# Strassen partial results accumulated in PSUM banks, mixer weights of layer 0 split ahead in gate and up, sums of squares on GpSimd: a two-layer hybrid decoder trunk

## The chip, the cores and the metric

One core of one Trainium2 chip. The metric is device time of one execution in microseconds (us), the median over several runs; lower is better. Float32 inputs and outputs.

## The reference

```python
for l in range(DEPTH):                      # DEPTH = 2, x is 512 tokens x 1024
    x = x + 0.5 * swiglu(rmsnorm(x, ffn1_norm[l]), ffn1_w_gate[l], ffn1_w_up[l], ffn1_w_down[l])
    proj = rmsnorm(x, mix_norm[l]) @ w_in[l]
    # four token mixers on column groups of proj: GLA, RG-LRU, RWKV-7, Mamba-2
    x = x + concatenate([y_gla, y_lru, y_rw, y_ssd]) @ w_out[l]
    x = x + 0.5 * swiglu(rmsnorm(x, ffn2_norm[l]), ffn2_w_gate[l], ffn2_w_up[l], ffn2_w_down[l])
return rmsnorm(x, final_norm)
# swiglu(x, g, u, d) = (silu(x @ g) * (x @ u)) @ d, 1024 -> 2816 -> 1024
```

## The kernel before, in words

The activations stay transposed: features on the 128 partitions, the 512 tokens along the free axis. The program is a straight line of FFN (0,0), mixers 0, FFN (0,1), FFN (1,0), mixers 1, FFN (1,1). Every large product is made of two 16-bit parts of each float32 operand, a rounded f16 part and a bf16 residue, in three matmuls (hi·hi, hi·lo, lo·hi). Splitting a weight tile takes an ACT cast (L245, f16) and a DVE subtraction (L214, bf16 residue).

**Gate and up** (`ffn`, L606). The 2816 hidden columns are cut in `NP` = 11 pairs of 128-column blocks. A pair `n`, for gate and up at once, is a 2x2 Strassen-Winograd product: seven half-size products of 24 matmuls of 128x256 (`product`, L564) in place of eight. Their operands are the weight blocks and sums of them: a11, a12, a22, s1, s2, s3, s4. The sums s1 and s3 come out of an accumulating DMA that GpSimd issues (`load_sums`, L532, tile `rb`); s2 and s4 are DVE additions in place in `ra`; `form` (L547) splits each into a tile `q`, of which there are `NQ` = 5. The activation operands `xf` are made once (`prep_forms`, L437).

Results lie in PSUM banks: `A` (a11, then a12 added by TensorE), `D` (a22), `B` (s2), `C` (s3), `E` (s1, then s4 added by TensorE). DVE forms the rest: `u2` = B − M1 (L722, M1 being an ACT copy of A after a11, L690), `u3` = u2 + C (L737), and the quarters of the tile `S`: u3 + D (L738), u3 + E (L679) and −E − u2 (`finish12`, L645). Then the row scale R, SiLU on ACT, the product and the split of `h`.

R comes from the sum of squares of x: eight ACT squares and seven DVE additions `acc<-acc,sq` (`prep_sum`, L460), a matmul with ones (`ns`), a power on GpSimd (`rtm`, L254), four transposes (`nb`) and an ACT copy to `R`. It runs beside the first products of an FFN.

**Down**: 16 half products of 33 matmuls of 128x512. Their weights `w` are loaded by SP, split into `ws` and used one tile later (`w_next`, L405). In its loop a generator `side` is advanced (L782): `pieces(l)` (L411) loads 512 columns of a mixer weight tile (`pw`), splits them (`ps`) and stores both parts to DRAM (`w_scr`), four pieces for each tile named in `AHEAD[l]`, the first two steps being loads alone. Such a tile is later loaded ready for use; the others are split in the mixers (`w_split`, L377) with two 128x1024 casts and subtractions.

**Mixers** (`mixers`, L1610): 17 weight tiles (`small`, `w1` to `w12` of the input projection, `w13` to `w16` of the output projection). Six generators and a `tail` of projections are interleaved at build time by a modelled `Clock` (L97) and the table `PACE`; a list scheduler then fixes each engine's order. `pre_ffn` (L575) loads and splits the first blocks of the next FFN. All engines run their own queue in order.

Of the kernel before, what the change touches and what calls it, by code (L numbers as in the profile page):

```python
# [35 lines left out]
AHEAD = (range(8, 15), range(3, 15))  # L36
# [130 lines left out]
def kernel(ctx: ExitStack, tc: tile.TileContext, xT, wffn, wmain, wdown, wsmall, pv_d, pr_d, sm_d, cn_d, outT):  # L167
# [292 lines left out]
    def prep_sum(k):  # L460
        if k == ORDER[0]:
            acc["t"] = slot("acc")
            ACT(acc["t"], x[k], AF.Square)
        else:
            s = slot("sq")
            ACT(s, x[k], AF.Square)
            TT(acc["t"], acc["t"], s, ADD)
# [138 lines left out]
    def ffn(l, ph, what, mid=None, keep=False, side=None, ahead=0):  # L606
# [5 lines left out]
        A, B, C, D, E, M1, U2, U3, S = {}, {}, {}, {}, {}, {}, {}, {}, {}  # L612
# [31 lines left out]
        def finish12(n):  # L644
            STT(quarter(n, 0, 1), gu(E.pop(n)), -1.0, gu(U2.pop(n)), MUL, SUB)  # L645
            scale_gate(n, 0)

        def sums(ks):
            for k in ks:
                prep_sum(k)  # L650

        for n in range(NP):
# [21 lines left out]
            if n == 1 and s == 0:  # L674
                R = norm_spread(r)
            A[n] = fbank("A")
            product(A[n], n, "a11", 0)
            if n - 1 in E:
                TT(quarter(n - 1, 1, 1), gu(U3.pop(n - 1)), gu(E[n - 1]), ADD)  # L679
                form(n - 1, "s4")  # L680
            if n == 0:
                load_sums(s, 1)
# [4 lines left out]
            D[n] = fbank("D")  # L687
            product(D[n], n, "a22", 3)
            M1[n] = slot("m1")
            acopy(out=M1[n], in_=A[n])  # L690
            if n > 0:
                scale_gate(n - 1, 1)
                activate(n - 1, 1, False)
            form(n, "a12")
            if n - 1 in E:
                product(E[n - 1], n - 1, "s4", 2, start=False)
            form(n, "s2")
            product(A[n], n, "a12", 1, start=False)
# [5 lines left out]
            if n == 0:  # L704
                sums(ORDER[0:4])
            B[n] = bank("B")
            product(B[n], n, "s2", 5)
            S[n] = wp.tile([128, 2048], F32, tag="w", name="S")
            acopy(out=quarter(n, 0, 0), in_=gu(A.pop(n)))
# [4 lines left out]
            if n == 0:  # L714
                sums(ORDER[4:8])
                r = norm_sum(1.0 / SX)
            if n == 2 and mid is not None:
                mid()
            C[n] = bank("C")
            product(C[n], n, "s3", 6)  # L720
            U2[n] = slot("u2")
            TT(U2[n], B.pop(n), M1.pop(n), SUB)  # L722
            if n + 2 < NP:
                load_sums(s, n + 2)
            elif not last:
                st["stage"] = s
                w_fill(stops[s] - 1, stops[s])
            if not last:
                form(n + 1, "a11")
            else:  # L730
                w_fill(stops[s], stops[s] + 1)
            E[n] = bank("E")
            product(E[n], n, "s1", 4)
            if n == 0:
# [1128 lines left out]
```

## Time and profile before

| | us |
|---|---|
| three runs | 1895.6, 1888.79, 1894.05 |
| median | 1894.05 |
| profiled execution | 1888.55 |
| its span, first to last instruction | 1886.8 |

| stage, us from the span's start | length | TensorE busy | VectorE busy |
|---|---|---|---|
| FFN (0,0), pairs 1 to 10: 49.81 to 226.10 | 176.29 | 176.29 | 163.73 |
| FFN (0,0), down: 230.59 to 344.18 | 113.59 | 112.67 | 65.46 |
| mixers of layer 0: 344.18 to 630.46 | 286.28 | 266.30 | 209.38 |
| mixers of layer 1: 1283.46 to 1546.88 | 263.42 | 260.73 | 195.78 |

The span is what the instructions of the profile cover; the execution's own time is 1.75 us more. Busy times are sums over instructions, and neighbours of a pipelined engine overlap a little, so an engine's instructions can start closer together than they last. In a row of the trace, the bracket at the end is the idle time ahead of it on its engine and what ended it. PE is TensorE, DVE VectorE, ACT ScalarE, POOL GpSimd, SP SyncE.

### The profile page before, as it was taken

The numbers are of one execution on the slowest core, as the hardware profiler recorded it, in microseconds if no ns is written. First come the engines' busy times: TensorE is split into PE (matmuls) and PEld (weight loads), VectorE is DVE, ScalarE is ACT, GpSimd is POOL, SyncE is SP. The second block draws the span as 40 slices with busy tenths as digits, with TensorE's granted clock in tenths as the row PEclk, the third lists the DMA queues.
The fourth block names the chain that finished last, engine by engine and source line by source line (L and its number), as shares of the span: only waits on it lengthen the run. The fifth ranks groups of instructions, "written<-read, shape, count | busy, mean of one in ns | idle before, by whom it ended". The sixth has DMA issues, their size and how long they took to land.

```text
span 1886.8 us, 33473 instructions
## 1 busy us (share of the span) xinstructions
PE 1811.9 (96%) x13758; PEld 1263.4 (67%) x13846; DVE 1463.4 (78%) x2389; ACT 901.3 (48%) x1404; POOL 77.2 (4%) x77
## 2 busy tenths in 40 slices
PE   6999999899998899999999999999999999999997
PEld 3888844346855588884468887444577558888544
DVE  8999964577877899996679998554777789999733
ACT  7555543443243655555455555444223456555520
POOL 0000000000000000000000000000000000000000
PEclk9999999899999999999999999999999999999999
DMA  8777367522142667736867672773212256774331
GB/s 299 207 207 211 90 216 259 195 90 78 31 138 63 196 181 211 199 111 223 269 214 217 192 207 92 223 261 136 89 37 68 101 145 192 212 203 131 108 108 45
DMA packets 113386, 304.43 MB, mean 161 GB/s; under 512 B 34512, under 2 KB 56016, under 8 KB 98128
## 3 DMA queue, kind: packets, MB, share of 16 engines
q1 hardware_dynamic: 107040, 257.19, 40.7%
q0 software_dynamic: 6192, 45.09, 12.4%
q8 instruction: 108, 1.77, 0.4%
q14 instruction: 46, 0.38, 0.1%
HBM read 272.87 MB, written 29.38 MB: 160 GB/s over the span
## 4 chain that ended last, share of the span: by engine, by line
PE 77%; DVE 9%; DMA 4%; issue 4%; ACT 4%; POOL 1%; SPq 1%; POOLq 0%; DVEq 0%; ACTq 0%
PE d L192 18%; PE A L192 11%; PE E L192 11%; PE pj L192 10%; PE C L192 5%; PE D L192 5%; PE B L192 5%; PE pt L192 3%; DMA w<-in_wdown_dram 2%; DVE ws L214 1%; DVE q L214 1%; PE wo L192 1%; DMA pw<-in_wmain_dram 1%; PE z L192 1%; PE go L192 1%
## 5 line engine op out<-in xcount | busy, mean ns | idle before, releaser
L192 PEld LDWEIGHTS <-q 128*128 128x128 f16 (+1 forms) x7320 | 717.0, 98 | 140.9 <-ACT q L245 24.5
L192 PEld LDWEIGHTS <-ws 128*128 128x128 f16 (+1 forms) x2802 | 274.5, 98 | 329.7 <-issue 23.1
L192 PE MATMUL d<-h,ws 128*128 128x512 f16 (+3 forms) x2135 | 456.6, 372 | 3.8 <-ACT h L245 1.6
L245 ACT CAST q<-ra 128x1024 f16<-128x1024 f32 (+1 forms) x177 | 181.6, 1030 | 209.2 <-PE E L192 110.8
L192 PE MATMUL A<-xf,q 128*128 128x256 f16 (+1 forms) x2064 | 244.8, 274 | 15.6 <-ACT q L245 10.6
L192 PE MATMUL E<-xf,q 128*128 128x256 f16 x2064 | 239.4, 273 | 3.3 <-DVE S L214 3.3
L214 DVE TENSOR_TENSOR ws<-w,ws 128x640 bf16<-128x640 f32 (+3 forms) x222 | 148.9, 710 | 92.6 <-ACT ws L245 91.6
L245 ACT CAST ws<-w 128x640 f16<-128x640 f32 (+3 forms) x222 | 127.6, 633 | 190.8 <-DMA w<-in_wdown_dram 69.3
L214 DVE TENSOR_TENSOR q<-ra,q 128x1024 bf16<-128x1024 f32 (+1 forms) x177 | 211.8, 1199 | 4.7 <-ACT q L245 4.6
L214 DVE TENSOR_TENSOR q<-rb,q 128x1024 bf16<-128x1024 f32 x88 | 107.5, 1223 | 31.1 <-ACT q L245 31.1
L192 PE MATMUL D<-xf,q 128*128 128x256 f16 (+1 forms) x1032 | 122.6, 273 | 2.5 <-ACT q L245 2.1
L192 PE MATMUL B<-xf,q 128*128 128x256 f16 (+1 forms) x1032 | 121.8, 274 | 1.1 <-ACT q L245 1.1
L192 PE MATMUL C<-xf,q 128*128 128x256 f16 (+1 forms) x1032 | 119.7, 273 | 0.0
L192 PEld LDWEIGHTS <-w 128*128 128x128 f16 (+1 forms) x672 | 64.3, 99 | 80.7 <-issue 14.1
L245 ACT CAST q<-rb 128x1024 f16<-128x1024 f32 x88 | 91.8, 1047 | 24.0 <-PE D L192 19.3
L192 PE MATMUL pj<-xh,w 128*128 128x512 f16 x320 | 102.0, 380 | 1.2
L192 PE MATMUL pj<-xh,ws 128*128 128x512 f16 x288 | 92.9, 393 | 5.6 <-ACT xh L241 4.9
L218 DVE SCALAR_TENSOR_TENSOR dx<-d,R 128x512 f32<-128x512 f32 (+1 forms) x33 | 22.2, 673 | 78.2 <-PE d L192 78.2
L241 ACT ACTIVATE th<-S 128x512 f32<-128x512 f32 x88 | 55.5, 631 | 47.4 <-DVE S L214 47.3
L536 POOL DMA_DIRECT2D rb<-in_wffn_dram x43 | 37.8, 880 | 806.1 <-DVE h L214 324.9
L214 DVE TENSOR_TENSOR ps<-pw,ps 128x512 bf16<-128x512 f32 x76 | 50.0, 687 | 26.4 <-ACT ps L245 24.7
L214 DVE TENSOR_TENSOR h<-hf,h 128x512 bf16<-128x512 f32 x88 | 57.9, 684 | 8.2 <-ACT h L245 8.2
(343 smaller groups left out, 2280.1 us busy)
## 6 DMA issues: line engine op xcount, KB each, us to landing
w<-in_wdown_dram SPq DMA_DIRECT2D x64, 704.0 KB, 4.2
ra<-in_wffn_dram SPq DMA_DIRECT2D x87, 512.0 KB, 4.8
rb<-in_wffn_dram SPq DMA_DIRECT2D x43, 1024.0 KB, 5.0
rb<-in_wffn_dram POOLq DMA_DIRECT2D x43, 1024.0 KB, 9.9
rc<-in_wffn_dram SPq DMA_DIRECT2D x43, 512.0 KB, 8.7
pw<-in_wmain_dram SPq DMA_DIRECT2D x76, 256.0 KB, 5.1
w_scr<-ps SPq DMA_DIRECT2D x76, 256.0 KB, 4.1
w<-w_scr SPq DMA_DIRECT2D x19, 1024.0 KB, 4.8
```

The lines of the kernel that those rows point to most:

```text
L192: PE.matmul(out, lhsT, rhs, start=start, stop=stop, skip_group_check=free)
L214: V.tensor_tensor(out=out, in0=in0, in1=in1, op=op)
L218: V.scalar_tensor_tensor(out=out, in0=in0, scalar=scalar, in1=in1, op0=op0, op1=op1)
L241: A.activation(out=out, in_=in_, func=func, scale=scale, bias=bias)
L245: A.copy(out=out, in_=in_)
L536: nc.gpsimd.dma_start(out=t, in_=wffn[s, n, :, 3072:5120], accum_op=ADD)
```

## The change

**Sums in banks.** Four banks are kept for a whole FFN: two for B (by n mod 2), one each for C and D. Four matmuls of 128x512 open them once per FFN. Then ACT copies −A (after a11) into B, on which TensorE adds s2; ACT copies B into C, on which s3 is added; C into D, on which a22 is added; and s4 is added on B, in the next pair. s1 goes into a bank of its own, which ACT copies to SBUF (`m5`). D is copied by ACT into its quarter of S. DVE keeps two of its five sums a pair, C + m5 and −B − m5. Counted from both programs for 43 pairs: 129 DVE additions of 128x512 fewer; 43 more each of the ACT copies C<-B, D<-C, S<-D, m<-E, while B<-A takes the place of m<-A. The order of the products changes, and a22 of a pair is formed inside its pair; since `pre_ffn` and the start of FFN (0,0) form it as well, it is formed twice in four places.

**Splits ahead.** `AHEAD[0]` grows by the tiles 3 to 7: 20 more pieces (load, ACT cast, DVE residue, store), 10 fewer casts and 10 fewer residues of 128x1024 in the mixers of layer 0, and five loads out of `w_scr`. In gate and up of FFN (0,0) `side` is advanced twice a pair, in those of FFN (1,0) once; 31 steps are left for the down of (0,0) (30 before), 12 for that of (1,0) (22 before).

**Sums of squares.** The seven additions at each FFN's start go from DVE to GpSimd; the 20 others stay.

Besides, small loads and derived constants move to other pairs, and `pre_ffn` runs earlier in the mixers.

```diff
-AHEAD = (range(8, 15), range(3, 15))
+AHEAD = (range(3, 15), range(3, 15))
...
-    def prep_sum(k):
+    def prep_sum(k, pool=False):
         if k == ORDER[0]:
             acc["t"] = slot("acc")
             ACT(acc["t"], x[k], AF.Square)
         else:
             s = slot("sq")
             ACT(s, x[k], AF.Square)
-            TT(acc["t"], acc["t"], s, ADD)
+            if pool:
+                GP.tensor_tensor(out=acc["t"], in0=acc["t"], in1=s, op=ADD)
+            else:
+                TT(acc["t"], acc["t"], s, ADD)
...
 
         def finish12(n):
-            STT(quarter(n, 0, 1), gu(E.pop(n)), -1.0, gu(U2.pop(n)), MUL, SUB)
+            STT(quarter(n, 0, 1), gu(B[n % 2]), -1.0, gu(E.pop(n)), MUL, SUB)
...
         def sums(ks):
             for k in ks:
-                prep_sum(k)
+                prep_sum(k, pool=True)
...
+            if n == 0:
+                load_sums(s, 1)
             A[n] = fbank("A")
+            if B is None:
+
+                B, C, D = [bank("B"), bank("B")], bank("C"), bank("D")
+                h, X = qs[n, "a11"][0], xf[0][0]
+                for t in (*B, C, D):
+                    mm(t, h[:, 0, 0:128], X[:, 0:2].rearrange("p n t -> p (n t)"))
             product(A[n], n, "a11", 0)
             if n - 1 in E:
-                TT(quarter(n - 1, 1, 1), gu(U3.pop(n - 1)), gu(E[n - 1]), ADD)
-                form(n - 1, "s4")
-            if n == 0:
-                load_sums(s, 1)
+                acopy(out=quarter(n - 1, 1, 0), in_=gu(D))
+                TT(quarter(n - 1, 1, 1), gu(C), gu(E[n - 1]), ADD)
+            form(n, "s2")
             if not last:
                 load_blocks(s, n + 1)
             else:
                 w_fill(stops[s] - 1, stops[s] + 1)
-            D[n] = fbank("D")
-            product(D[n], n, "a22", 3)
-            M1[n] = slot("m1")
-            acopy(out=M1[n], in_=A[n])
+            if n - 1 in E:
+                product(B[(n - 1) % 2], n - 1, "s4", 2, start=False)
+            ACT(B[n % 2], A[n], AF.Copy, scale=-1.0)
             if n > 0:
                 scale_gate(n - 1, 1)
-                activate(n - 1, 1, False)
             form(n, "a12")
-            if n - 1 in E:
-                product(E[n - 1], n - 1, "s4", 2, start=False)
-            form(n, "s2")
-            product(A[n], n, "a12", 1, start=False)
+            product(B[n % 2], n, "s2", 5, start=False)
             form(n, "s3")
             if n - 1 in E:
                 finish12(n - 1)
             elif n > 0:
                 scale_gate(n - 1, 0)
-            if n == 0:
+            if n > 0:
+                activate(n - 1, 1, False)
+            else:
                 sums(ORDER[0:4])
-            B[n] = bank("B")
-            product(B[n], n, "s2", 5)
-            S[n] = wp.tile([128, 2048], F32, tag="w", name="S")
-            acopy(out=quarter(n, 0, 0), in_=gu(A.pop(n)))
+            product(A[n], n, "a12", 1, start=False)
+            acopy(out=C, in_=B[n % 2])
             form(n, "s1")
             if n > 0:
                 activate(n - 1, 0, True)
                 S.pop(n - 1)
-            if n == 0:
+            else:
                 sums(ORDER[4:8])
                 r = norm_sum(1.0 / SX)
-            if n == 2 and mid is not None:
+            if n == 6 and mid is not None:
                 mid()
-            C[n] = bank("C")
-            product(C[n], n, "s3", 6)
-            U2[n] = slot("u2")
-            TT(U2[n], B.pop(n), M1.pop(n), SUB)
+            product(C, n, "s3", 6, start=False)
+            S[n] = wp.tile([128, 2048], F32, tag="w", name="S")
+            acopy(out=quarter(n, 0, 0), in_=gu(A.pop(n)))
+            form(n, "a22")
             if n + 2 < NP:
                 load_sums(s, n + 2)
             elif not last:
                 st["stage"] = s
                 w_fill(stops[s] - 1, stops[s])
+            if n > 0 and ahead:
+                next(side, None)
+            m5 = fbank("E")
+            product(m5, n, "s1", 4)
+            acopy(out=D, in_=C)
+            if n == 0:
+                R = norm_spread(r)
             if not last:
                 form(n + 1, "a11")
+                if n > 0 and ahead > 1:
+                    next(side, None)
+            else:
+                form(n, "s4")
+            product(D, n, "a22", 3, start=False)
+            E[n] = slot("m5")
+            acopy(out=E[n], in_=m5)
+            if not last:
+                form(n, "s4")
             else:
                 w_fill(stops[s], stops[s] + 1)
-            E[n] = bank("E")
-            product(E[n], n, "s1", 4)
-            if n == 0:
-                R = norm_spread(r)
-            U3[n] = slot("u3")
-            TT(U3[n], U2[n], C.pop(n), ADD)
-            TT(quarter(n, 1, 0), gu(U3[n]), gu(D.pop(n)), ADD)
...
-                    for _ in range(2 + ahead * q):
+                    for _ in range(2 + (keep and q)):
                         next(side, None)
+                if i == 2 and q == 0 and mid2 is not None:
+                    mid2()
...
+                            if kh == 1 and m == 0 and n == 1:
+                                open_ffn()
+                                pre_ffn(2 * l + 1, 0)
-                        if m == 0:
-                            open_ffn()
-                            pre_ffn(2 * l + 1, 0)
-                        if mh == 1 and i == 2:
+                        if mh == 0 and i == 3:
                             pre_ffn(2 * l + 1, 1)
                         prep_k(l, 1, m)
...
-    for l in range(DEPTH):
-        ffn(l, 0, "mix", mid1 if l == 0 else None, keep=True, side=split_ahead[l], ahead=1)
-        mixers(l)
-
-        def mid2():
-            load_small(l + 1)
-            derive_norm(l + 1)
-            derive(l + 1)
-        ffn(l, 1, 0 if l + 1 < DEPTH else None, mid2 if l + 1 < DEPTH else None,
-            side=split_ahead[l + 1] if l + 1 < DEPTH else None)
+    ffn(0, 0, "mix", small0, lambda: derive(0), keep=True, side=split_ahead[0], ahead=2)
+    mixers(0)
+    ffn(0, 1, 0, norms1, side=split_ahead[1])
+    ffn(1, 0, "mix", lambda: load_small(1), lambda: derive(1), keep=True, side=split_ahead[1], ahead=1)
+    mixers(1)
+    ffn(1, 1, None)
     leave("ext", "xfp")
```

ACT, one pair of gate and up in the middle of an FFN. Before (FFN (0,0)); q is a split operand, th the SiLU, S the quarters, h the hidden values:

```order
110 L245 COPY m_2097<-A 128x512
111 L245 CAST q<-rb 128x1024
112 L241 ACTIVATE th<-S 128x512
113 L245 CAST q<-rb 128x1024
114 L245 CAST q<-ra 128x1024
115 L241 ACTIVATE th<-S 128x512
116 L245 COPY S<-A 128x2x256
117 L245 CAST h<-hf 128x512
118 L245 CAST q<-rc 128x1024
119 L245 CAST q<-ra 128x1024 x3
```

and now (FFN (0,1)); B, C, D, E and A are PSUM banks:

```order
466 L241 ACTIVATE th<-S 128x512
467 L241 ACTIVATE B<-A 128x512
468 L245 CAST q<-rb 128x1024
469 L245 CAST q<-rc 128x1024
470 L241 ACTIVATE th<-S 128x512
471 L245 COPY C<-B 128x512
472 L245 CAST h<-hf 128x512
473 L245 CAST q<-ra 128x1024
474 L245 COPY S<-A 128x2x256
475 L245 CAST q<-ra 128x1024
476 L245 COPY D<-C 128x512
477 L245 CAST q<-ra 128x1024
```

Between the casts stand the copies from bank to bank, each behind the casts that TensorE needs next.

GpSimd, from the end of the mixers of layer 0 to the end of gate and up in FFN (1,0). Before, rb being the accumulating loads and rtm the power:

```order
17 L254 TENSOR_TENSOR rs<-ss,cn_t 128x8 x2
18 L254 TENSOR_TENSOR rs<-var,cn_t 128x8
19 L536 DMA rb<-in_wffn_dram 128x2048 x3
20 L254 TENSOR_TENSOR rtm<-ms,cn_t 128x4
21 L536 DMA rb<-in_wffn_dram 128x2048 x11
```

and now:

```order
21 L254 TENSOR_TENSOR rs<-var,cn_t 128x8
22 L539 DMA rb<-in_wffn_dram 128x2048 x2
23 L468 TENSOR_TENSOR acc<-acc,sq 128x512 x7
24 L254 TENSOR_TENSOR rtm<-ms,cn_t 128x4
25 L539 DMA rb<-in_wffn_dram 128x2048 x11
```

The seven additions stand ahead of the power, and the third load of the FFN now stands behind both.

ACT, from the end of the down of FFN (0,0) into the mixers of layer 0. Before; ws are the splits of mixer tiles, xh and sq belong to the last two blocks of x, R<-nb is the row scale:

```order
194 L245 CAST ws<-w 128x512 x2
195 L245 CAST ws<-w 128x1024 x2
196 L241 ACTIVATE xh<-x,der_78 128x512
197 L241 ACTIVATE sq<-x 128x512
198 L245 CAST ws<-w 128x1024 x4
199 L241 ACTIVATE xh<-x,der_78 128x512
200 L241 ACTIVATE sq<-x 128x512
201 L245 CAST ws<-w 128x1024 x2
202 L245 COPY R<-nb 128x512
```

and now, ps being a piece split ahead:

```order
262 L245 CAST ws<-w 128x512 x2
263 L245 CAST ws<-w 128x1024 x2
264 L241 ACTIVATE xh<-x,der_78 128x512
265 L241 ACTIVATE sq<-x 128x512
266 L245 CAST ps<-pw 128x512
267 L245 CAST ws<-w 128x1024 x2
268 L241 ACTIVATE xh<-x,der_78 128x512
269 L241 ACTIVATE sq<-x 128x512
270 L245 COPY R<-nb 128x512
```

Of the four split tiles of two halves, w1 and w2 are left (263 and 267), and a last piece stands between them.

## Rows read from the trace of the kernel before

**Rows 1.** The page: span, busy time and share of each engine.

```profile
span 1886.8 us, 33473 instructions
PE 1811.9 (96%) x13758; PEld 1263.4 (67%) x13846; DVE 1463.4 (78%) x2389; ACT 901.3 (48%) x1404; POOL 77.2 (4%) x77
```

**Rows 2.** Windows, gate and up of FFN (0,0), one pair of FFN (0,1).

```profile
core 0: us, PE busy (x) PEld busy (x) DVE busy (x) ACT busy (x) POOL busy (x), PEclk, DMA share, GB/s
49.81:226.10 176.29, 176.29 (x1608) 157.65 (x1606) 163.73 (x215) 101.12 (x128) 6.98 (x8) 0.99 0.65 186
676.59:694.93 18.34, 18.34 (x171) 16.44 (x168) 18.27 (x22) 9.65 (x12) 0.87 (x1) 1.00 0.83 232
```

**Rows 3.** Windows, the mixers: layer 0, layer 1, their first 27.8 us, their later parts.

```profile
344.18:630.46 286.28, 266.30 (x2121) 164.60 (x2140) 209.38 (x472) 112.04 (x211) 14.28 (x10) 0.96 0.31 97
1283.46:1546.88 263.42, 260.73 (x2125) 161.51 (x2148) 195.78 (x462) 99.68 (x197) 13.59 (x10) 1.00 0.29 89
...
344.18:372.00 27.82, 20.66 (x73) 9.15 (x74) 15.24 (x19) 11.45 (x14) 1.04 (x1) 0.75 0.59 214
1283.46:1311.30 27.84, 27.68 (x120) 12.46 (x122) 11.11 (x18) 13.53 (x20) 1.03 (x1) 1.00 0.39 138
470.00:620.00 150.00, 137.61 (x1378) 94.45 (x1387) 113.52 (x264) 51.22 (x106) 9.48 (x7) 0.98 0.27 79
1400.00:1536.00 136.00, 133.94 (x1342) 90.83 (x1353) 107.48 (x251) 51.20 (x105) 9.48 (x7) 1.00 0.25 78
```

**Rows 4.** Windows, the start of FFN (0,1), up to its pair 2.

```profile
630.46:676.59 46.13, 38.77 (x326) 31.90 (x324) 42.58 (x69) 29.79 (x42) 3.73 (x3) 0.96 0.62 180
```

**Rows 5.** Timeline of PE in one pair: start, length, engine, line, what.

```profile
134.40 2.78 PE L192 MATMUL A<-xf,q 128*128 128x256 f16 x24
...
152.74 0.93 PE L192 MATMUL A<-xf,q 128*128 128x256 f16 x7
```

**Rows 6.** Timeline of ACT in the same pair.

```profile
137.22 0.58 ACT L245 COPY m<-A 128x512 f32<-128x512 f32 x1 [1.53 <-PE A L192]
...
142.50 1.04 ACT L245 CAST q<-ra 128x1024 f16<-128x1024 f32 x1 [1.56 <-PE E L192]
```

**Rows 7.** Timeline of ACT at the start of the mixers of layer 0.

```profile
346.58 1.99 ACT L245 CAST ws<-w 128x1024 f16<-128x1024 f32 x2 [7.77 <-DMA w<-in_wmain_dram]
...
354.83 1.99 ACT L245 CAST ws<-w 128x1024 f16<-128x1024 f32 x2 [3.24 <-DMA w<-in_wmain_dram]
...
369.36 0.58 ACT L245 COPY R<-nb 128x512 f32<-128x512 f32 x1 [7.29 <-PE nb L197]
```

**Rows 8.** The same copy at the start of the mixers of layer 1.

```profile
1295.26 0.58 ACT L245 COPY R<-nb 128x512 f32<-128x512 f32 x1 [8.91 <-PE nb L197]
```

**Rows 9.** Groups of DVE in the mixers of layer 0, the costliest.

```profile
L214 DVE TENSOR_TENSOR ws<-w,ws 128x1024 bf16<-128x1024 f32 x18 | 21.4, 1219 | 8.5 <-ACT ws L245 8.4
```

**Rows 10.** Waits of PE from 470 to 620 us: total, times, longest.

```profile
PE wo L192 <- DVE y L218: 3.7, 1, 3.7
PE yt L197 <- DVE sc L218: 2.8, 1, 2.8
```

**Rows 11.** Timeline of DVE at the start of FFN (0,1).

```profile
643.02 0.68 DVE L214 TENSOR_TENSOR acc<-acc,sq 128x512 f32<-128x512 f32 x1
...
652.90 0.68 DVE L214 TENSOR_TENSOR acc<-acc,sq 128x512 f32<-128x512 f32 x1
...
655.89 1.22 DVE L214 TENSOR_TENSOR ra<-ra,rb 128x1024 f32<-128x1024 f32 x1
```

**Rows 12.** Timeline of POOL, the power of FFN (0,1).

```profile
656.06 1.95 POOL L254 TENSOR_TENSOR rtm<-ms,cn_t 128x4 f32<-128x4 f32 x1 [11.25 <-DVE ms L225]
```

**Rows 13.** The same power at the start of the mixers of layer 0.

```profile
361.81 1.04 POOL L254 TENSOR_TENSOR rtm<-ms,cn_t 128x4 f32<-128x4 f32 x1 [128.47 <-DVE ms L225]
```

**Rows 14.** Groups of POOL over the whole span.

```profile
L1131 POOL COPY zb<-cn_t 64x256 f32<-64x256 f32 x4 | 1.5, 389 | 0.0
```

More of the change, by code (lines that the diff above doesn't have):

```diff
@@ L604, in direct, with ffn @@
         return p
-    def ffn(l, ph, what, mid=None, keep=False, side=None, ahead=0):
+    def ffn(l, ph, what, mid=None, mid2=None, keep=False, side=None, ahead=0):
         nonlocal xh, xl, ext, xfp
@@ L611, in ffn @@
         R = r = None
-        A, B, C, D, E, M1, U2, U3, S = {}, {}, {}, {}, {}, {}, {}, {}, {}
+        A, E, S = {}, {}, {}
+        B = C = D = None
         def gu(t):
@@ L727, in ffn @@
                 w_fill(stops[s] - 1, stops[s])
+            if n > 0 and ahead:
[5 more added lines that the diff above has]
+                R = norm_spread(r)
             if not last:
                 form(n + 1, "a11")
+                if n > 0 and ahead > 1:
[7 more added lines that the diff above has]
+                form(n, "s4")
             else:
                 w_fill(stops[s], stops[s] + 1)
-            E[n] = bank("E")
-            product(E[n], n, "s1", 4)
-            if n == 0:
-                R = norm_spread(r)
-            U3[n] = slot("u3")
-            TT(U3[n], U2[n], C.pop(n), ADD)
-            TT(quarter(n, 1, 0), gu(U3[n]), gu(D.pop(n)), ADD)
-            if not last:
-                form(n + 1, "a22")
-            else:
-                form(n, "s4")
         n = NP - 1
-        TT(quarter(n, 1, 1), gu(U3.pop(n)), gu(E[n]), ADD)
-        product(E[n], n, "s4", 2, start=False)
+        TT(quarter(n, 1, 1), gu(C), gu(E[n]), ADD)
+        product(B[n % 2], n, "s4", 2, start=False)
+        acopy(out=quarter(n, 1, 0), in_=gu(D))
         if what == "mix":
@@ L1724, with small0 @@
     dma(out=cn_t, in_=cn_d)
-    def mid1():
-        dma(out=pv_t[1], in_=pv_d[1])
+    def small0():
         load_small(0)
@@ L1734, in mid1, with norms1 @@
                 dma(out=bass.AP(t.tensor, o, [[520, 128], [1, n]]), in_=zz[:, 0:n])
-        derive(0)
+    def norms1():
+        dma(out=pv_t[1], in_=pv_d[1])
+        derive_norm(1)
     split_ahead = [pieces(l) for l in range(DEPTH)]
-    for l in range(DEPTH):
-        ffn(l, 0, "mix", mid1 if l == 0 else None, keep=True, side=split_ahead[l], ahead=1)
-        mixers(l)
-        def mid2():
-            load_small(l + 1)
-            derive_norm(l + 1)
-            derive(l + 1)
-        ffn(l, 1, 0 if l + 1 < DEPTH else None, mid2 if l + 1 < DEPTH else None,
-            side=split_ahead[l + 1] if l + 1 < DEPTH else None)
+    ffn(0, 0, "mix", small0, lambda: derive(0), keep=True, side=split_ahead[0], ahead=2)
[4 more added lines that the diff above has]
+    ffn(1, 1, None)
     leave("ext", "xfp")
```

## The prediction

> **What bounds the kernel now.** I read the page first, then the windows, then the timelines of the stretches where TensorE is not busy all the time. The page says that PE is busy for 1811.9 of 1886.8 us [rows 1]: only some 75 us can be won without giving PE less work, and the change gives it slightly more. So the question is where those 75 us lie. Not in gate and up: a pair takes 18.34 us, PE is busy for all of it [rows 2], and its seven products start every 2.62 us ((152.74 − 134.40) / 7) [rows 5]. DVE is close behind there (18.27 busy), but it holds nobody up.
>
> The idle time lies in two kinds of places. In the mixers of layer 0 PE idles 286.28 − 266.30 = 20.0 us, in those of layer 1 2.7 us, with nearly the same number of matmuls, and the granted clock is 0.96 against 1.00 [rows 3]; layer 0 takes 22.9 us longer. And in the start of an FFN, 13 products, worth 13 x 2.62 = 34.1 us, take 46.13 in FFN (0,1), with DVE busy for 42.58 of it [rows 4]. Layer 1 already has its tiles 3 to 14 split ahead, so it shows what layer 0 might become.
>
> **The change part by part.**
>
> *Mixers of layer 0.* Ten residues of 1.22 us on DVE [rows 9] and ten casts of 1.04 us on ACT (a cast of the same size in [rows 6]) leave the stage. What that is worth has two parts. In the first 27.8 us layer 0 gets through 73 matmul records, layer 1 through 120, and PE's clock is 0.75 against 1.00 [rows 3]: after each gap it works for a while at the lower of its two levels, 1.2 instead of 2.4 GHz. What ends ACT's waits there are loads of mixer tiles, 7.77 and 3.24 us, and R is copied 25.2 us into the stage (369.36 − 344.18), against 11.8 in layer 1 (1295.26 − 1283.46) [rows 7, 8]. The change takes away w3 and w4, but w1 and w2 are still loaded raw, behind the last pieces, since 31 steps of `side` are left for the down where there were 30. So the first wait of 7.77 stays, and I give the change only about the second, 3.24: −3. In the later part, 150.00 us of layer 0 stand against 136.00 of layer 1, with 12.4 and 2.1 us idle [rows 3]; the waits are single ones on DVE's latency, 3.7 for y, 2.8 for sc [rows 10]. With the splits gone, the order of layer 0 becomes nearly that of layer 1, the projections last longer as filler, and DVE is 12.2 us freer: −12 of the 14. Together −15. Bounds: the whole difference to layer 1, −23, and half, −8; that nothing comes is a rival.
>
> *Sums in banks, steady pairs.* ACT gains four copies of 0.58 us a pair [rows 6]: 9.65 + 2.3 = 12.0 us of 18.34. DVE sheds three additions of 0.68 (the size of [rows 11]): 18.27 − 2.0. Each copy lies between two products on the same bank, with one other product of 2.62 us between them: s4 of the last pair beside −A to B, a12 beside B to C, s1 beside C to D. One cast may stand ahead of the copy on ACT: 1.04 + 0.58 = 1.6, which leaves 1.0 us. So nothing. Below nothing it can't be, as PE has no gap there to give back; above, it is a rival.
>
> *The pieces in gate and up.* In FFN (0,0) two a pair: ACT +1.2 us and DVE +1.4, at about 0.6 and 0.7 each, as the 128x512 copies and additions above. Both fit (13.2 and 17.7 of 18.34). Their load and store add 4 x 0.26 MB in 18.34 us, 57 GB/s to 186; a pair at 232 GB/s ran without a gap [rows 2], and 243 is near. Nothing. If a piece's load came late, ACT would wait in its queue ahead of the next bank copy: that goes to the rival on stalls. The downs: one step more in (0,0), ten fewer in (1,0); nothing. Five tiles come from DRAM already split, no larger than the raw ones that they replace; nothing.
>
> *The FFN starts.* Four opening matmuls cost 4 x 0.22 us (2.62 / 24 for 256 columns, twice that for 512), 3.5 us over four FFNs if nothing hides them; PE waits in the starts anyhow (46.13 − 38.77 in [rows 4]), so I take +2 of 0 to 3.5. Forming a22 twice costs DVE 1.22 us a start. The additions are the unknown. On DVE they stood 1.65 us apart ((652.90 − 643.02) / 6) [rows 11], between other work. An addition of 128x512 on POOL is not in the trace. From below: a copy of 256 columns takes 0.39 us [rows 14], so 512 take 0.8. From above: two inputs, 1.6, and a wait as that of the power in FFN (0,1), which was under way for 1.95 us beside a DVE addition of 1.22 that began 0.17 us before it, and took 1.04 where DVE did nothing [rows 11, 12, 13]; with 0.9 of wait that is 2.5. Under 1.65 us an addition the sum isn't later than before and DVE is 7 x 0.68 − 1.22 = 3.5 us freer a start; at 2.5 R is 7 x 0.85 = 6 us late. That lateness counts in full, since DVE's `ms<-ns` now stands ahead of the split of a22 and of the next a11 in its queue, and PE's `ns` ahead of the end of C. I take the middle, 1.65, and no gain, since what DVE is freed of can be lost to that blocking: 0, from −14 to +24 over four FFNs. The third `rb` load now stands behind the additions on POOL's queue, but is not needed for two pairs, 36 us; nothing.
>
> *Sum.* −15 + 0 + 0 + 2 = −13 from the profiled 1888.55: 1875.5. That execution is 5.5 us under the median of the three runs (1894.05), which spread over 7 us; so I put the median of the changed kernel 1.5 higher: **1877**, and call a time within 0.5% of 1894.05 (1884.6 to 1903.5) no change, about what a measurement of this kernel can tell.
>
> **The rivals.**
>
> *GpSimd and DVE keep each other out (the other side).* Place: the starts. For: the power waited for a DVE addition with two inputs in SBUF; nearly all of DVE's work there is such; DVE is busy for 42.58 of 46.13 us [rows 4, 11, 12]. If that holds in both directions, each POOL addition of c us takes c from DVE in place of 0.68, so a start costs 7c − 4.8 + 1.2 us more, if DVE sets its end. At c = 1.2 that is 4.8 a start, 19 in all: 1894.5, no change. It decides from c = 1.5: (7 x 1.5 − 3.6) x 4 = 28 brings 1903.5. At 2.0 it is 42: 1917, slower. Against: not all of DVE's waits in a start are PE's, and no row shows DVE waiting for POOL's port. Chance 0.16, half of it slower.
> The Trainium skill has such a rule: by "SBUF — State Buffer", section "Who interferes with whom", a DVE instruction with two SBUF inputs contends with a GpSimd one that reads SBUF, and whoever comes first keeps the shared ports for its whole instruction; the power's 1.95 against 1.04 us agrees for one direction, and no run here shows the other. The "GPSIMD Engine Reference", section 3.1, gives 4497 ns for an addition of 2048 columns, from which an estimate for 512 is 1.12 us; by it the rival comes to 1892.
>
> *The copies stall PE.* Three seeds a pair lie on PE's path if ACT is late. For: ACT serves casts, copies and pieces in one queue, and a wait there on a late load holds up the next seed. Against: 1.0 us of slack and ACT at two thirds. At 0.5 us a seed, 3 x 43 x 0.5 = 64: 1940, slower. Chance 0.06.
>
> *Layer 0 gains nothing.* The start of its mixers is bound by the loads of w1 and w2, and its later gaps by chains of latency under its own `PACE` table, not by DVE's load: 1875.5 + 15 = 1890, no change. For: the waits in [rows 10] are one each. Against: layer 1. Chance 0.14.
>
> *Everything comes.* Layer 0 becomes layer 1 (−23) and each start gives 2 to 3 us (−9), openings hidden: 1857. Chance 0.17.
>
> **How the numbers follow.** The forecast, 1866 to 1884 by itself, has 0.46; 0.01 is left for a mix that ends at no change. Faster by over 0.5%: 0.46 + 0.17 = 0.63. No change: 0.14 + 0.08 + 0.01 = 0.23. Slower: 0.08 + 0.06 = 0.14. The range from 1855 to 1895 takes in the forecast, nearly all of "everything comes", "layer 0 gains nothing" and the mild half of the first rival, and leaves out the slower cases and the far ends of the others, about 0.2.
>
> **What would show it.** Right: the mixers of layer 0 near 271 us with PE idle under 8; a pair of gate and up still 18.34 with no wait of PE for a bank copy; the starts within 2 us of before, POOL's additions about 1.65 us apart. Wrong: a wait of `B`, `C` or `D` for ACT in every pair (the copies stall); starts over 48 us, with additions of over 1.5 us and DVE instructions beside them longer than before (the first rival); a first stretch of the mixers with the clock still at 0.75 and the later gaps still on y and sc (layer 0 gains nothing).

## The result and the profile after

The changed kernel takes 1913.24 us (median of four runs, 1910.58 to 1916.71) against 1894.82 before: slower, at a ratio of 1.0105 (95% interval 1.0077 to 1.0132). The prediction was 1877 and its range ended at 1895, so it was wrong in size and in sign. The profiled execution took 1912.54 us; that of the kernel before, 1888.55 us, lay some 6 us under its median, so what is measured from it comes out some 6 us too high.

The page of the changed kernel, span and busy times, the counterpart of [rows 1]:

```profile
span 1910.7 us, 33761 instructions
PE 1828.8 (96%) x13862; PEld 1273.1 (67%) x13862; DVE 1390.9 (73%) x2246; ACT 993.1 (52%) x1592; POOL 124.7 (7%) x105
```

DVE lost 72 us of work, ACT gained 92, POOL 47, and PE is busy 17 us longer with hardly more to do: part of its matmuls ran at the lower clock (mean granted clock 0.978, before 0.99).

The windows of the changed kernel: one pair of FFN (0,1), the start of FFN (0,1) up to the first product of its pair 2 (13 products besides the openings, as in [rows 4]), the mixers of layer 0, their first 27.8 us and their later part. They answer to [rows 2], [rows 4] and [rows 3].

```profile
core 0: us, PE busy (x) PEld busy (x) DVE busy (x) ACT busy (x) POOL busy (x), PEclk, DMA share, GB/s
681.64:700.00 18.36, 18.36 (x170) 16.45 (x169) 15.26 (x17) 12.03 (x16) 1.54 (x2) 1.00 0.78 232
634.97:684.28 49.31, 40.48 (x329) 34.27 (x328) 37.52 (x45) 33.34 (x47) 13.77 (x10) 0.90 0.59 172
353.02:634.97 281.95, 266.90 (x2142) 162.90 (x2142) 202.96 (x468) 104.27 (x203) 14.30 (x10) 0.96 0.34 106
353.02:380.84 27.82, 17.07 (x56) 7.16 (x56) 12.08 (x18) 7.29 (x10) 1.04 (x1) 0.69 0.85 292
470.00:620.00 150.00, 146.22 (x1484) 100.06 (x1483) 117.02 (x274) 51.97 (x110) 8.56 (x6) 1.00 0.25 78
```

The steady pair is as long as it was and PE never waits in it. In the start DVE has 5 us less to do than before (37.52 for 42.58), yet the same 13 products take 3.2 us longer (49.31 for 46.13), and the granted clock fell from 0.96 to 0.90. The mixers of layer 0 are 4.3 us shorter: their later part gained (146.2 us busy of 150, before 137.6), their first part lost (56 matmul records, before 73).

The waits of PE over the whole span of the changed kernel: total, times, longest. The 13.2 us are the program's beginning, as before.

```profile
PE ns L192 <- POOL acc L468: 26.8, 4, 10.3
PE g L192 <- ACT xd L241: 13.2, 1, 13.2
PE pj L192 <- ACT xh L241: 9.2, 2, 7.9
PE B L192 <- ACT B L241: 6.6, 3, 3.0
```

The first row is new. Once in each FFN, PE stands for POOL's additions. The last row is PE waiting for the copy of −A into B, at three starts.

Stage by stage, from the first matmul of a stage to that of the next (a stage of an FFN holds start, gate and up, and down), in us. The rows after the first are differences from before; the e rows are the experiments below, all from one profiled execution each.

| | FFN (0,0) | mixers 0 | FFN (0,1) | FFN (1,0) | mixers 1 | FFN (1,1), end | span |
|---|---|---|---|---|---|---|---|
| before | 344.2 | 286.3 | 329.3 | 323.7 | 263.4 | 339.9 | 1886.8 |
| after | +8.8 | −4.3 | +2.2 | +7.9 | +2.2 | +7.1 | 1910.7 |
| e1, additions on DVE | +7.9 | −5.6 | −5.8 | −0.9 | 0.0 | +3.3 | 1885.6 |
| e2, norm later | +9.3 | −6.1 | −0.9 | +4.9 | 0.0 | +6.5 | 1900.5 |
| e3, before, additions on POOL | +2.8 | +0.7 | +5.5 | +7.0 | +1.9 | +8.1 | 1912.9 |
| e4, three pieces | +10.5 | −21.0 | +1.6 | +8.4 | +2.2 | +10.3 | 1898.8 |
| e5, e1 and e4 | +13.4 | −22.7 | −4.9 | +1.1 | 0.0 | +3.3 | 1877.0 |
| e6, e5 and constants early | +9.6 | −21.4 | −5.5 | −1.1 | +2.2 | −0.3 | 1870.3 |
| e7, before, splits ahead | +8.4 | −20.9 | +0.2 | +0.1 | 0.0 | +2.3 | 1876.9 |
| e8, banks alone | +4.7 | −2.0 | −4.7 | −1.2 | +0.8 | −1.2 | 1883.2 |
| e9, three steps in the down | +4.1 | −17.6 | −4.1 | −1.3 | 0.0 | +3.3 | 1871.1 |

### The profile page after: what moved, and what is told of

The parts are those of the page before. It is cut to its first block, busy times and chain, and to the rows that moved or that the text cites. A ratio compares the mean times of both kernels' runs of the same rounds, so it can differ in the third digit from the quotient of the medians.

```text
span 1910.7 us, 33761 instructions
## 1 busy us (share of the span) xinstructions
PE 1828.8 (96%) x13862; PEld 1273.1 (67%) x13862; DVE 1390.9 (73%) x2246; ACT 993.1 (52%) x1592; POOL 124.7 (7%) x105
## 4 chain that ended last, share of the span: by engine, by line
PE 75%; DVE 8%; DMA 5%; issue 4%; ACT 3%; POOL 2%; SPq 1%; POOLq 0%; DVEq 0%; ACTq 0%
PE d L192 17%; PE B L192 11%; PE A L192 10%; PE pj L192 9%; PE E L192 6%; PE D L192 5%; PE C L192 5%; PE pt L192 3%; DMA w<-in_wdown_dram 2%; POOL acc L468 2%; DVE ws L214 1%; PE wo L192 1%; DMA pw<-in_wmain_dram 1%; PE go L192 1%; PE z L192 1%
## 5 line engine op out<-in xcount | busy, mean ns | idle before, releaser
L192 PEld LDWEIGHTS <-ws 128*128 128x128 f16 (+1 forms) x2610 | 255.8, 98 | 313.3 <-issue 26.2
L192 PE MATMUL B<-xf,q 128*128 128x256 f16 (+2 forms) x2072 | 241.2, 276 | 7.3 <-ACT B L241 6.6
L192 PE MATMUL A<-xf,q 128*128 128x256 f16 x2064 | 240.9, 273 | 1.2 <-ACT xf L241 0.8
L192 PEld LDWEIGHTS <-w 128*128 128x128 f16 (+1 forms) x864 | 82.6, 99 | 98.1 <-issue 11.8
L192 PE MATMUL pj<-xh,w 128*128 128x512 f16 x448 | 144.0, 384 | 0.0
L192 PE MATMUL E<-xf,q 128*128 128x256 f16 (+1 forms) x1032 | 125.7, 280 | 1.0 <-DVE q L214 1.0
L192 PE MATMUL C<-xf,q 128*128 128x256 f16 (+2 forms) x1036 | 123.5, 275 | 0.3 <-ACT C L245 0.3
L192 PE MATMUL D<-xf,q 128*128 128x256 f16 (+2 forms) x1036 | 121.5, 273 | 0.0
L192 PE MATMUL pj<-xl,w 128*128 128x512 bf16 x224 | 85.9, 383 | 0.0
L214 DVE TENSOR_TENSOR ps<-pw,ps 128x512 bf16<-128x512 f32 x96 | 63.2, 687 | 21.2 <-ACT ps L245 20.7
```

The source lines that it names most:

```text
L192: PE.matmul(out, lhsT, rhs, start=start, stop=stop, skip_group_check=free)
L214: V.tensor_tensor(out=out, in0=in0, in1=in1, op=op)
```

## The experiments

Two theories came out of the comparison. **P**: GpSimd's additions set the end of the four starts. **Q**: at the start of the mixers of layer 0, SP's queue holds the loads of w1 and w2 behind the last pieces. Their rival **S** was that the new order of products, the opening matmuls and the bank copies cost the starts. All results are medians of repeated runs, with the ratio to the kernel before and its 95% interval.

**e1, the additions back on DVE.**

```diff
         def sums(ks):
             for k in ks:
-                prep_sum(k, pool=True)
+                prep_sum(k)
```

> The changed kernel with the seven additions of each FFN start back on DVE, nothing else edited. In the changed kernel PE waits 10.3, 5.7, 5.9 and 4.9 us at the sum of squares of the four FFNs, and the clock is at its lower level just after. Theory P (GpSimd's additions set the end of the starts): these four waits go and with them most of the 24 us that the gate and up parts got longer; 1892 to 1898. Rival S (the new order of products, the opening matmuls and the bank copies cost the starts): the starts stay as long, 1908 to 1915.

1887.4 us, ratio 0.9967 (0.9958 to 0.9977): 26 us less than the changed kernel, more than P asked for, and faster than before. S falls as the main cause. Of the four waits, three shrink to under 1 us; FFN (0,0) keeps one of 4.5 us. The start of FFN (0,1), the same 13 products, takes 41.30 us at full clock:

```profile
632.72:674.02 41.30, 37.16 (x330) 32.08 (x329) 38.30 (x52) 32.95 (x47) 2.82 (x2) 1.00 0.63 192
```

This is PE at the two ends of the norm in FFN (0,1) of this run:

```profile
653.13 1.02 PE L192 MATMUL ns<-ones,acc 128*128 128x1 f32 x8 [0.79 <-DVE acc L214]
...
656.85 0.60 PE L197 MATMUL nb<-cn_t,rtm 128*128 128x128 f32 x4
```

**e2, the norm later.** The additions stay on GpSimd; only the place of the norm moves (in FFN (0,0), which has a path of its own, nothing does).

```diff
             product(A[n], n, "a11", 0)
+            if n == 1 and s > 0:
+                R = norm_spread(r)
...
                 sums(ORDER[4:8])
-                r = norm_sum(1.0 / SX)
...
             acopy(out=D, in_=C)
-            if n == 0:
-                R = norm_spread(r)
...
             product(D, n, "a22", 3, start=False)
+            if n == 0:
+                r = norm_sum(1.0 / SX)
```

> The changed kernel, additions still on GpSimd, but the sum with ones stands behind the product of a22 on PE and the scale behind the next pair's first splits on DVE, some 2 products later. If the harm of the additions is that PE and DVE stand still in their queues behind a late sum (theory P1), the four waits of PE go although the additions last as long: 1893 to 1899, as the run with the additions on DVE. If the harm is that DVE and GpSimd keep each other out of SBUF (theory P2), DVE's doubled instructions stay and little is won: 1906 to 1912. Rival S: 1908 to 1915.

1900.95 us, ratio 1.0028 (1.0016 to 1.0041): 12 less than the changed kernel, 13.5 more than e1. That is about half, but in the profiles, 10.2 us apart, only 6.2 of it lie in the FFNs (26.0 − 19.8), where e1 takes back 21.5; 4.0 came in the mixers, where nothing was edited. So between a third and a half of the harm goes when less stands behind the late sum, and the rest stays. The sum itself still ends late, as POOL and PE in FFN (0,1) of this run show:

```profile
644.41 14.06 POOL L468 TENSOR_TENSOR acc<-acc,sq 128x512 f32<-128x512 f32 x7 [11.70 <-ACT sq L241]
```

```profile
658.52 1.12 PE L192 MATMUL ns<-ones,acc 128*128 128x1 f32 x8 [2.55 <-POOL acc L468]
```

With DVE busy nearly all through, the seven additions take 14.1 us instead of 11.5, and PE still waits for them, 2.2 to 3.5 us in each of the three FFNs that the edit touches. So P1's condition, that these waits go, was not met, and neither P1's nor P2's forecast came. That both act is a reading which fits, not shown; what is left was not split between the late sum and DVE's own delays.

**e3, the kernel before with its additions on GpSimd.**

```diff
-            TT(acc["t"], acc["t"], s, ADD)
+            if pool:
+                GP.tensor_tensor(out=acc["t"], in0=acc["t"], in1=s, op=ADD)
+            else:
+                TT(acc["t"], acc["t"], s, ADD)
...
         def sums(ks):
             for k in ks:
-                prep_sum(k)
+                prep_sum(k, pool=True)
```

> The kernel before with the seven additions of each FFN start on GpSimd, nothing else. Theory P: it becomes slower by 8 to 20 us, 1903 to 1915, with PE waiting at the sum of squares in all four FFNs. Rival S: within 4 us of before, 1891 to 1899, since DVE is relieved by 28 additions there as well.

1913.99 us, ratio 1.0110 (1.0094 to 1.0125), at the upper end of P's forecast. This one edit, alone, costs 19.6 us, as much as the whole change. PE in FFN (0,1) of this run:

```profile
657.79 1.86 PE L192 MATMUL ns<-ones,acc 128*128 128x1 f32 x8 [7.56 <-POOL acc L468]
```

**e4, three pieces a pair in gate and up of FFN (0,0).**

```diff
                 form(n + 1, "a11")
-                if n > 0 and ahead > 1:
-                    next(side, None)
+                if n > 0:
+                    for _ in range(ahead - 1):
+                        next(side, None)
...
-    ffn(0, 0, "mix", small0, lambda: derive(0), keep=True, side=split_ahead[0], ahead=2)
+    ffn(0, 0, "mix", small0, lambda: derive(0), keep=True, side=split_ahead[0], ahead=3)
```

> The changed kernel with three pieces a pair in gate and up of FFN (0,0) in place of two, so that the last pieces are done before the last tile loads of the down and w1 and w2 are issued behind the x_keep store of block 6, without pieces ahead of them. If the order of SP's queue sets the 7.9 us wait of PE at the start of the mixers of layer 0 (theory Q), it shrinks to under 3 us and the clock there rises: 6 to 10 us less than the changed kernel, 1903 to 1907. If DMA bandwidth or the down itself sets it, or the pieces now stall gate and up, no change or slower, 1911 to 1918.

1900.1 us, ratio 1.0033 (1.0016 to 1.0050): 13 less than the changed kernel. Q holds, and by more than it asked for. The queue of SP in the changed kernel, where the mixers begin at 353.02 us (x_keep is the store of a block of x that the down has finished, pw and w_scr the load and the store of a piece):

```profile
346.30 0.33 SPq L249 DMA_DIRECT2D x_keep<-x  x1
346.68 1.40 SPq L249 DMA_DIRECT2D pw<-in_wmain_dram  x3
349.10 3.22 SPq L249 DMA_DIRECT2D w_scr<-ps  x3
352.38 0.60 SPq L249 DMA_DIRECT2D pw<-in_wmain_dram  x1
353.03 0.45 SPq L249 DMA_DIRECT2D w<-in_wmain_dram  x1
```

and in e4, where they begin at 354.71:

```profile
337.21 0.33 SPq L249 DMA_DIRECT2D x_keep<-x  x1
338.15 3.33 SPq L249 DMA_DIRECT2D w<-in_wmain_dram  x2
342.48 0.33 SPq L249 DMA_DIRECT2D x_keep<-x  x1
```

w1 is issued as the mixers begin in the one, 16.6 us ahead of them in the other. In the kernel before it was issued 5.0 us ahead of them (339.17 for 344.18, by the same view):

```profile
339.17 1.10 SPq L249 DMA_DIRECT2D w<-in_wmain_dram  x2
```

The stage is now that of layer 1, 265.3 us, and in its first 27.8 us PE is busy throughout, at full clock:

```profile
354.71:620.02 265.31, 260.64 (x2118) 162.70 (x2140) 193.81 (x456) 98.17 (x195) 14.28 (x10) 0.99 0.30 93
354.71:382.53 27.82, 27.71 (x125) 13.10 (x126) 12.13 (x32) 10.64 (x21) 1.04 (x1) 1.00 0.39 143
```

**e5, both edits together** (e1 and e4).

> Additions back on DVE and three pieces a pair, together. If the two faults are separate places (starts and the start of the mixers of layer 0), their gains add: 1887 - 13 = 1874, 1870 to 1878. If the pieces of the third step meet the 28 additions on DVE, or a piece waits in ACT's queue, less: 1879 to 1886.

1876.76 us, ratio 0.9913 (0.9894 to 0.9931). The gains add, nearly: 10.6 of e4's 13. The third piece is not free: FFN (0,0) is 5.5 us longer than in e1. In its start DVE waits, as it did in e1, for a small load ahead of most of its additions:

```profile
40.87 0.24 DVE L223 TENSOR_SCALAR der<-pv 128x8 f32<-128x8 f32 x2 [2.70 <-DMA pv<-in_pv_dram]
```

**e6, that load early.** The constants of layer 1 (`pv`) are used in FFN (0,1) by the program's text, but the scheduler had put their derivation into the start of FFN (0,0).

```diff
     dma(out=pv_t[0], in_=pv_d[0])
+    dma(out=pv_t[1], in_=pv_d[1])
...
     def norms1():
-        dma(out=pv_t[1], in_=pv_d[1])
         derive_norm(1)
```

> As the run of both (additions on DVE, three pieces a pair), and the load of the second layer's column constants issued as the second load of the program instead of behind the first FFN's weights. In the run with the additions on DVE, DVE stood 3.4 us in FFN (0,0) for that load, ahead of the additions and of the splits of pair 1. If that wait lies on PE's path (theory W), 3 to 6 us less than the run of both; if ACT's casts or the weight loads end last there, the same within 2 us.

1870.85 us, ratio 0.9886 (0.9868 to 0.9903): 6 less than e5, at the upper end of what W expected. FFN (0,0) accounts for 3.8 of it. This version beats both kernels, by 23 us the one before.

**e7, the kernel before with the splits ahead alone.** `AHEAD[0]` as in the change, three pieces a pair.

```diff
-AHEAD = (range(8, 15), range(3, 15))
+AHEAD = (range(3, 15), range(3, 15))
...
+            if n > 0 and ahead:
+                next(side, None)
             if not last:
                 form(n + 1, "a11")
+                if n > 0:
+                    for _ in range(ahead - 1):
+                        next(side, None)
...
-                    for _ in range(2 + ahead * q):
+                    for _ in range(2 + (keep and q)):
...
-        ffn(l, 0, "mix", mid1 if l == 0 else None, keep=True, side=split_ahead[l], ahead=1)
+        ffn(l, 0, "mix", mid1 if l == 0 else None, keep=True, side=split_ahead[l], ahead=3 if l == 0 else 0)
```

> The kernel before with the splits ahead alone: tiles 3 to 7 of layer 0 too, three pieces a pair in gate and up of FFN (0,0); sums on DVE, additions on DVE. The mixers of layer 0 should gain 14 to 21 us. If DVE has no room in gate and up (18.27 of 18.34 us a pair are busy, three residues of 0.69 come to it; theory M: the bank sums are what makes the room), PE waits some 1 us a pair there, 10 to 15 in all: 1884 to 1892. If the overlap of DVE's instructions leaves the room (rival), 1874 to 1880, and the bank sums are not needed.

1878.56 us, ratio 0.9920 (0.9903 to 0.9936). M falls: PE waited once in gate and up, for ACT, not a little in every pair, though DVE's summed busy time, which holds overlap, is 175 of 184 us. But the room was not free. These pairs take 184.10 us where they took 176.29 [rows 2], FFN (0,0) as a whole 8.4 more, and the one wait came of a piece whose load was late, while ACT stood in its queue ahead of the copy that PE needed:

```profile
50.30:234.40 184.10, 178.54 (x1608) 158.69 (x1607) 175.24 (x239) 113.36 (x152) 6.98 (x8) 0.98 0.85 254
```

```profile
PE A L192 <- ACT m L245: 5.6, 1, 5.6
```

```profile
89.26 0.62 ACT L245 CAST ps<-pw 128x512 f16<-128x512 f32 x1 [7.06 <-DMA pw<-in_wmain_dram]
```

**e8, the sums in banks alone**, with the small moves that came with the change. e1, and layer 0 split as before.

```diff
-AHEAD = (range(3, 15), range(3, 15))
+AHEAD = (range(8, 15), range(3, 15))
...
-    ffn(0, 0, "mix", small0, lambda: derive(0), keep=True, side=split_ahead[0], ahead=2)
+    ffn(0, 0, "mix", small0, lambda: derive(0), keep=True, side=split_ahead[0], ahead=0)
```

> The sums in banks alone: the changed kernel with the additions on DVE and layer 0 split as before (tiles 8 to 14, all pieces in the down). If the bank copies cost PE nothing and gain nothing in steady pairs, 1886 to 1894, with the mixers of layer 0 at 285 to 288 us. If the new order of products helps or harms the starts by itself: under 1884 or over 1897.

1891.91 us, ratio 0.9988 (0.9975 to 1.0001): no change that could be told. By stage it loses 4.7 in FFN (0,0) and gains as much in FFN (0,1). The loss has a part that is not the banks': DVE waits there for the same small load as in e5, a wait that the kernel before and e7 do not have.

```profile
40.40 0.25 DVE L223 TENSOR_SCALAR der<-pv 128x8 f32<-128x8 f32 x2 [2.55 <-DMA pv<-in_pv_dram]
```

Where neither kernel has this wait, and both have three pieces a pair and the additions on DVE, e6 with the banks and the small moves is 7.7 us faster than e7 without them; FFN (0,1) accounts for 5.7 of it.

**e9, three steps in the down.** e1 and the early constants, two pieces a pair as in the change.

```diff
-                    for _ in range(2 + (keep and q)):
+                    for _ in range(3 if keep else 2):
                         next(side, None)
```

> Additions on DVE, the column constants loaded early, two pieces a pair in gate and up of FFN (0,0) as in the changed kernel, but three steps a half product in the downs of FFN (0,0) and (1,0) instead of two and three, so that the pieces end a block earlier without a third one in gate and up. Theory Q (the place of w1 and w2 in SP's queue is all that counts): the mixers of layer 0 at 264 to 268 us as with three a pair, gate and up 2 to 5 us cheaper than there: 1866 to 1869. If the third step's pieces in the down crowd out the tile loads of the down: 1871 to 1880.

1871.28 us, ratio 0.9872 (0.9852 to 0.9892): above what Q expected, at the lower end of its rival, and equal to e6. FFN (0,0) is 5.5 us cheaper than there, but the mixers of layer 0 gain 17.6 instead of 21.4, and FFN (1,1) is 3.6 us longer, which nothing in the edit explains. w1 is issued 8.7 us ahead of the mixers, which begin at 348.25, between e4 and the kernel before:

```profile
339.57 0.33 SPq L249 DMA_DIRECT2D w<-in_wmain_dram  x1
```

**e10, a22 of the first pair formed once** (e9, without the second forming).

```diff
         else:
             form(0, "a11")
-            form(0, "a22")
...
                 load_sums(s, 2)
-                form(1, "a22")
```

> As the run before it in this pair, and a22 of an FFN's first pair formed once. If the second forming (1.04 us of ACT, 1.22 us of DVE at each of four starts) lies on the path, 2 to 5 us less than that run; if other work hides it, within 1.5 us of it.

1871.27 us, ratio 0.9874 (0.9856 to 0.9893): the same as e9. Other work hides the second forming.

## Why the prediction was wrong

**What bounds the kernel: right.** Steady pairs gave nothing and took nothing; the time lay in the mixers of layer 0 and in the starts. Against the forecast of 1875.5 the profiled execution is 37 us long: 24 in the FFNs (26 for 2), 11 in the mixers of layer 0 (−4.3 for −15), 2 in those of layer 1.

**Sums in banks, steady pairs: right.** ACT's busy time in a pair is 12.03 us, forecast 12.0, and PE has no wait. One pair of ACT in FFN (0,1) of the changed kernel:

```profile
692.40 0.57 ACT L245 COPY C<-B 128x512 f32<-128x512 f32 x1 [0.51 <-PE B L192]
...
697.64 0.57 ACT L245 COPY D<-C 128x512 f32<-128x512 f32 x1 [1.14 <-PE C L192]
```

Each copy starts at once when its product ends, and has 2.62 us. In steady pairs the rival that the copies stall PE appeared only where three pieces a pair load ACT: in e6, PE waits for the copy into D twice, 1.4 us each. At the starts PE does wait for the copy into B, 6.6 us in three FFNs of the changed kernel.

**The FFN starts: the step that failed.** The prediction put the starts at +2, with POOL's additions at 1.65 us and no net cost, saying that under 1.65 us an addition "the sum isn't later than before". The price was right in three FFNs of four (11.4 to 11.8 us for seven additions; in FFN (0,0) they took 18.3), and the conclusion wrong. That the price hit was partly luck: it was the middle of two bounds, and an addition takes 1.26 us alone and 2.13 beside DVE. POOL in the start of FFN (0,1) of the changed kernel:

```profile
645.54 11.45 POOL L468 TENSOR_TENSOR acc<-acc,sq 128x512 f32<-128x512 f32 x7 [11.41 <-ACT sq L241]
659.18 1.04 POOL L254 TENSOR_TENSOR rtm<-ms,cn_t 128x4 f32<-128x4 f32 x1 [2.20 <-DVE ms L225]
```

11.45 us for seven is 1.64 each, and the chain ends 22.0 us into the FFN (656.99 − 634.97), where DVE's ended 23.1 us into it before (653.58 − 630.46, [rows 4, 11]). So here the sum is even a little earlier; in the other FFNs it ends 4.7, 0.5 and 0.7 us later. But before, DVE made its additions between the splits that PE needs next, and when it came to the norm those were done. PE too came to its norm after the sum, 24.3 us into the FFN:

```profile
654.71 0.95 PE L192 MATMUL ns<-ones,acc 128*128 128x1 f32 x8
```

Now both come to the norm early, PE 16.4 us into the FFN, and stand there, DVE with the splits behind it. DVE and PE in the same start:

```profile
648.20 2.29 DVE L214 TENSOR_TENSOR q<-rb,q 128x1024 bf16<-128x1024 f32 x1
658.94 0.16 DVE L225 TENSOR_SCALAR ms<-ns 128x4 f32<-128x4 f32 x1 [8.44 <-PE ns L192]
```

```profile
657.03 1.87 PE L192 MATMUL ns<-ones,acc 128*128 128x1 f32 x8 [5.67 <-POOL acc L468]
```

DVE idles 8.4 us with the splits of a22 and of the next a11 behind its wait; PE idles 5.7 us and then needs those splits; and the clock is 0.90 over the start. The prediction named this order of DVE's queue, but only as a price for a late sum. The price falls due for a sum that is as early as before as well: what counts is when the queues reach it. DVE has to wait out POOL's whole chain, from the end of what stands ahead of `ms<-ns`, and whatever it did meanwhile before is now late. With the additions back on DVE the four FFN stages are 4.5 us longer than before, in the changed kernel 26.0: the term that was put at 0, from −14 to +24, measured 21.5: 8.0, 8.8 and 3.8 in FFN (0,1), (1,0) and (1,1), and 0.9 in FFN (0,0). There PE's wait of 10.3 us is not its cost: without the additions on GpSimd, in e1, other waits take its place.

**The first rival** named this place and the way: GpSimd and DVE keep each other out. Its sign came too, a start of over 48 us (49.31) with DVE instructions longer than before. The rows show both directions, the second of which no row of before showed. POOL's second addition, beside DVE's work, and the last one, with DVE idle, in FFN (0,1) of the changed kernel:

```profile
647.28 2.13 POOL L468 TENSOR_TENSOR acc<-acc,sq 128x512 f32<-128x512 f32 x1
...
655.72 1.26 POOL L468 TENSOR_TENSOR acc<-acc,sq 128x512 f32<-128x512 f32 x1
```

DVE's split, in the fence above, takes 2.29 us beside POOL; an instruction of that size takes 1.22 alone [rows 11]. The trace agrees, in both directions, with the rule that the prediction took from the Trainium skill, "SBUF — State Buffer", section "Who interferes with whom". The estimate of 1.12 us for an addition, from the Trainium skill, "GPSIMD Engine Reference", section 3.1, comes out a little under the 1.26 measured alone. With 1.26 us, the rival's sum is (7 x 1.26 − 3.6) x 4 = 21 us, near the 21.5 measured; but that the size fits doesn't make exclusion the whole cause, since a third to a half of it goes in e2, where the additions still stand on GpSimd.

**Mixers of layer 0: the second error, in size.** −15 was forecast, −4.3 came. The later part behaved: PE is busy 8.6 us more of the same 150, for 12 forecast. The first part was to gain 3 and lost instead. ACT in the changed kernel, which answers to [rows 7]:

```profile
360.66 1.99 ACT L245 CAST ws<-w 128x1024 f16<-128x1024 f32 x2 [7.22 <-DMA w<-in_wmain_dram]
...
381.88 0.59 ACT L245 COPY R<-nb 128x512 f32<-128x512 f32 x1 [11.05 <-PE nb L197]
```

The wait of ACT stayed (7.22, before 7.77), as forecast, but its end moved from 2.4 to 7.6 us into the stage, and R is copied 28.9 us in, before 25.2. The step that failed is "one step more in (0,0)", put at nothing. Of the 30 steps of before, the first two only load, so its down splits 28 pieces; with two steps a pair done in gate and up, the 31 that are left split 31. And a piece is not free there. SP's queue in the changed kernel, from one x_keep store to the next, with five pieces between them,

```profile
310.26 0.33 SPq L249 DMA_DIRECT2D x_keep<-x  x1
...
328.47 0.33 SPq L249 DMA_DIRECT2D x_keep<-x  x1
...
346.30 0.33 SPq L249 DMA_DIRECT2D x_keep<-x  x1
```

takes 18 us a block, where PE takes 14.2 (113.6 / 8), as in the kernel before (17.8, from 279.88 to 297.70). For much of it SP stands at the x_keep store, for DVE's `x` (24.1 us in three blocks), which comes behind the split of a tile of the down, whose load SP issued behind the pieces. So the queue falls behind PE by some 4 us a block as long as pieces last, and hands its delay to w1; in e4 the last stores, with no full set of pieces between them, follow 7.5 and 5.3 us apart. "Everything comes", −23 for the mixers of layer 0, was within reach: nine steps moved from the down to gate and up (e4, e5, e6, e7) or the third step in the down (e9, e10) get 17 to 23 of it. The price is in FFN (0,0), where the prediction put the pieces at nothing: two a pair cost some 3 us (e1 beside e8, one profile each), the third 5.5 more (e5 beside e1, e6 beside e9).

**Smaller terms.** The second forming of a22, which the prediction charged to DVE's time in a start, costs nothing (e10). With the additions on DVE the start of FFN (0,1) gains 4.8 us by the sums in banks and the small moves (41.30 in e1 for 46.13), where the prediction had only the openings, at +2 in all; which of the two it is was not tried. A small load for a later FFN, whose use the scheduler had moved in among FFN (0,0)'s additions, was not seen; it costs 3.8 us (e6).

**Left open.** How the part of POOL's harm that e2 leaves divides between the late sum and DVE's doubled instructions; and 2.2 us of mixers 1, which some runs show and some do not, whatever their edit.

## What to carry to other kernels

Work moved to an idle engine is paid for by whoever waits for its result: before giving GpSimd part of a chain, find where the result is waited for in each engine's queue, and price everything behind that wait, not the operation. Where a producer of loads shares one queue with the loads of the next stage, its last items can decide when that stage starts, as here; look at issue times in that queue, not at bandwidth alone, and end the producer early enough for the queue to catch up. And take a bundle of edits apart: here one of three cost 20 us (e3), one, with a third piece a pair, was worth 15 (e7), one, with the small moves, some 8 (e6 beside e7), though by itself next to nothing (e8), and their sum hid all of it.

## What the runs showed of the hardware that was not expected

DVE can shut GpSimd out for much longer than one instruction. POOL in the start of FFN (0,0) of the changed kernel:

```profile
30.57 8.37 POOL L468 TENSOR_TENSOR acc<-acc,sq 128x512 f32<-128x512 f32 x1 [8.30 <-ACT sq L241]
```

and DVE's last instruction with two inputs in SBUF ahead of its end:

```profile
36.59 1.22 DVE L214 TENSOR_TENSOR ra<-ra,rb 128x1024 f32<-128x1024 f32 x1
37.92 3.19 DVE L223 TENSOR_SCALAR der<-pv 128x8 f32<-128x8 f32 x5
```

The addition waited 7.1 us (8.37 − 1.26) through DVE's unbroken row of such instructions and ended 1.1 us after the last of them. It is not a price of the program's first addition alone: in e3 the first one of FFN (0,1) took 4.66 us and also ended 1.1 us after such a row. In FFN (0,1) of the changed kernel the two engines took turns. Why one start has turns and the other not, the runs do not tell. The tiny DVE instructions on 128x8 that follow suffered too: five of them took 3.19 us beside POOL's additions (two of the five, 1.04 and 2.02, nearly all of it), in the kernel before two took 0.24.

```profile
38.28 0.24 DVE L223 TENSOR_SCALAR der<-pv 128x8 f32<-128x8 f32 x2
```
